# A two-layer retention and latent-attention trunk on one core: x's HBM copy, the place of the sines, the place of the scores, and two jobs moved from VectorE to ScalarE

## The chip, the core and the metric

The kernel runs on one core of a Trainium2 chip. The core has a matrix engine (TensorE), a vector engine (VectorE), an engine for activation functions and scaled copies (ScalarE), a general engine (GpSimd), and a queue that issues most transfers (SyncE, called SP in the profile). They run beside each other, each works through its own instructions in order, and they wait for one another with semaphores. In the profile they are PE (with PEld for its weight loads), ACT, DVE, POOL and SP. The metric is the time of one execution on the device in microseconds. The kernel before was run three times: 2519.52, 2520.91 and 2526.63 us, so the median is 2520.91 us.

## The reference, cut to what matters

The input x has 256 rows of 2048 numbers (float32). Two layers follow each other, and each is followed by an MLP of width 8192.

```python
# layer 0: retention, 8 heads, qk 256, v 512
h = rms_norm(x, norm_mix[0])
q, k, v, gate = split(h @ w_in)
q, k = apply_rope(q, cos, sin), apply_rope(k, cos, sin) * 256**-0.5
o = (q @ k.T * decay) @ v                 # written by chunks in the reference
o = o * rsqrt(mean(o * o) + eps)
x = x + (silu(gate) * o) @ w_out
x = x + square(relu(rms_norm(x) @ w1)) @ w2
# layer 1: latent attention, 16 heads, 128 plain + 64 rotary columns
k_nope, k_pe, v = mla_shared_kv(rms_norm(x, kv_norm_in), ...)
q = rms_norm(h @ w_dq) @ w_uq             # then split, normed, rotary part turned
sc = (q_nope @ k_nope.T + q_pe @ k_pe.T) * 192**-0.5      # causal mask
x = x + softmax(sc) @ v @ w_o
x = x + square(relu(rms_norm(x) @ w1)) @ w2
```

The angles of the rotation are positions times fixed frequencies; their sines and cosines are computed on the chip.

## The kernel before

All weights are float32 and are streamed from HBM once. Each float32 factor of a product is split into a rounded part (`wh`) and a remainder (`wl`): `split` rounds by a copy on ScalarE (L167, or L170 with a scale) and subtracts on VectorE (L168, L171). A product then is three matmuls: high by high, high by low, low by high. `stream` (and `quad` for the large products, which uses a seven-product scheme for some blocks) loads one chunk of a weight on SP into one of 3 `raw` buffers, splits it into two halves of 1024 columns, and issues the matmuls. There are 5 buffers for each kind of half. So the chain for each half is SP, ScalarE, VectorE, TensorE.

Work beside the weight stream is put off with `later(n, fn)`: `fn` runs when n more chunks have been issued (a chunk is one tick of `clock`), and `tick` calls what is due. The framework's scheduler then gives each engine its order from the order of issue and from its own estimate of when operands are ready; so an instruction can stand earlier on its engine than where it was written. Small tiles of 2 KB per partition come from one pool, `f2k`, with 14 buffers; whoever takes a buffer waits for the last reader of its former content.

The start runs as follows. `start(half)` is called for each half of the first weight (gate of head 0, `rg`); it loads two blocks of the transposed x (`x0t`) and splits them into `act0`, scaled by the norm's gain. The norm's row scale isn't known yet: the first products are made without it, and the rotation tables and gates take it up. At half 5, `ret_tables` lets GpSimd compute the reduced angles (`sincos`, L465 to L501: `tr_ang` to `tr_rr`, some twenty instructions). At half 7 the following is put off: `load_x` loads x itself in eight tiles of 128x512 on SP (`x0`) and squares them on ScalarE (`square_sum`, L162); `scale_tables` (`later(5)`) makes the row scales `r0` (sums on VectorE, power on GpSimd, L145 and L147), takes the sines of the angles on ScalarE (L505), multiplies them by `r0` (`tr_scaled`, L540) and transposes them on TensorE (`tr_tp`) into `rope_tab`; `mla_tables` takes the sines of the second layer's angles (`tm`); and eight copies of x from HBM to HBM (`xh`, the running x's home) are issued by GpSimd (L594).

For each head h, `ret_projected` streams the query and the key weights (`rq`, `rk`, 2 chunks each). `ret_rope` adds the two parts of the product (L600, L601) and later rotates (`rotate`, L607 to L611); `ret_scores` later multiplies keys by queries (`sc`, L626), multiplies by the decay (`st`, L628 and L629) and splits (`sh`, `sl`). Head 0's values (`rv`, 4 chunks) come next, and for later heads gate and values together (`rp`, 8 chunks); then `ret_out` multiplies the split scores with the split values (`vh`, `vl`, L170 and L171). Head 0 has to wait for the tables, so its rotations, scores and gate are put off by more ticks (`wait`, L679).

In layer 1, the query stage streams `uq` in three chunks for each of eight pairs of heads. `query` copies the product from PSUM with the row scale (`qs`, ScalarE, L942), squares it (`qu`, VectorE, L944), sums the squares (L945, L946), norms and turns; after transposes (`qntp`, `qptp`), `score` multiplies with the keys, masks (L999), takes the maximum (L1004), the exponential with its sum (ScalarE, L1009), the reciprocal (L1010) and multiplies by it (VectorE, L1015). Its result is transposed (`ptp`) and multiplied by the values (`ao`), and the output product `wo` follows.

Of the kernel before, what the change touches and what calls it, by code (L numbers as in the profile page):

```python
# [15 lines left out]
AF = mybir.ActivationFunctionType  # L16
ALU = mybir.AluOpType
# [4 lines left out]
NT = 2  # L22
# [3 lines left out]
NB = 4  # L26
# [24 lines left out]
def yoco(ctx: ExitStack, tc: tile.TileContext, a):  # L51
# [7 lines left out]
    def small(w, name):  # L59
        return pool.tile([P, w], F32, tag="small", bufs=36, name=name)  # L60
# [20 lines left out]
    def later(n, fn):  # L81
        queue.append((clock[0] + n, next(count), fn))
# [77 lines left out]
    def square_sum(src, acc, name):  # L160
        junk = pool.tile([P, 512], BF16, tag="junk", bufs=1, name=f"{name}_sq")
        nc.scalar.activation(junk[:, : src.free_size()], src, AF.Square, accum_out=acc)  # L162
# [302 lines left out]
    def sincos(inv, w, name):  # L465

        n = NT * w

        def f2k(shape, name):
            return shaped(act_tile(name, F32).rearrange("p j i s -> p (j i s)"), shape)  # L470

        ang = f2k([NT, w], f"{name}_ang")
        for t in range(NT):
            nc.gpsimd.tensor_scalar(ang[:, t], inv, pos_f[:, t : t + 1], None, op0=ALU.mult)
        flat = ang.rearrange("p t w -> p (t w)")
        k = f2k([2, n], f"{name}_k")
        for i in range(2):
            nc.gpsimd.tensor_scalar(k[:, i], flat, 1 / (2 * PI), 0.25 * i, op0=ALU.mult, op1=ALU.add)
        nc.gpsimd.tensor_scalar(k, k, MAGIC, -MAGIC, op0=ALU.add, op1=ALU.add)
        kh = f2k([2, n], f"{name}_kh")  # L480
        nc.gpsimd.tensor_scalar(kh, k, MAGIC_HI, -MAGIC_HI, op0=ALU.add, op1=ALU.add)
        kl = f2k([2, n], f"{name}_kl")
        nc.gpsimd.tensor_tensor(kl, k, kh, op=ALU.subtract)
        r = f2k([2, n], f"{name}_rr")
        both = flat.unsqueeze(1).to_broadcast([P, 2, n])
        part = f2k([2, n], f"{name}_part")

        def less(dst, src, kk, c):
            nc.gpsimd.tensor_scalar(part, kk, c, None, op0=ALU.mult)
            nc.gpsimd.tensor_tensor(dst, src, part, op=ALU.subtract)  # L490

        less(r, both, kh, c1)
        for kk, c in ((kl, c1), (kh, c2), (kl, c2), (k, c3)):
            less(r, r, kk, c)
        nc.gpsimd.tensor_scalar(r[:, 1], r[:, 1], PI / 2, None, op0=ALU.add)
        nc.gpsimd.tensor_scalar(k, r, 1 / (2 * PI), MAGIC, op0=ALU.mult, op1=ALU.add)
        nc.gpsimd.tensor_scalar(k, k, -MAGIC, None, op0=ALU.add)
        for c in (c1, c2 + c3):
            less(r, r, k, c)
        lim = 3.1415925  # L500
        nc.gpsimd.tensor_scalar(r, r, lim, -lim, op0=ALU.min, op1=ALU.max)  # L501

        def finish():
            sc = f2k([2, n], f"{name}_sc")
            nc.scalar.activation(sc, r, AF.Sin)  # L505
            return sc.rearrange("p i (t w) -> p i t w", t=NT)

        return finish
# [4 lines left out]
    gqn = pool.tile([P, 1], F32, name="gqn")  # L513

    def mla_tables():
        sm = mla_sc[0]()
        for t in range(NT):
            for i, s in ((0, 1.0), (1, scale)):
                tab = pe_tabs[t][i]
                g = gpe[:, i * ROPE : (i + 1) * ROPE]  # L520
                for half in range(2):
                    cols = slice(half * 32, half * 32 + 32)
                    other = slice(32 - half * 32, 64 - half * 32)
                    nc.vector.scalar_tensor_tensor(
                        tab[:, 0, cols], sm[:, 1, t], s, g[:, cols], op0=ALU.mult, op1=ALU.mult
                    )
                    nc.vector.scalar_tensor_tensor(
                        tab[:, 1, cols], sm[:, 0, t], s * (2 * half - 1), g[:, other], op0=ALU.mult, op1=ALU.mult
                    )
# [4 lines left out]

    def scale_tables():
        r0.extend(x_rstd(ss0, "n0"))
        sc = ret_sc[0]()
        scaled = f2k([2, NT, P], "tr_scaled")
        for t in range(NT):
            nc.vector.tensor_scalar(scaled[:, :, t], sc[:, :, t], r0[t], None, op0=ALU.mult)  # L540

        def turn():
            nc.scalar.copy(rope_tab, transposed(lambda t, j: scaled[:, j, t], "tr_tp"))

        later(2, turn)


    act0, sums0, r0, ret_sc, mla_sc = [], [], [], [], []

    def first_inputs(c):  # L550

# [17 lines left out]
    def x_in(t, b):  # L569
        return a["x"][t * P : (t + 1) * P, b * 512 : (b + 1) * 512]  # L570

    def load_x(b):
        for t in range(NT):
            x0 = f2k([512], f"x0_{t}{b}")
            nc.sync.dma_start(x0, x_in(t, b))
            square_sum(x0, ss0[t][:, b : b + 1], f"n0_{t}{b}")

    def start(half):
        first_inputs(half)
        if half == 3:  # L580
            nc.sync.dma_start(pos_i, a["pos"])
            nc.sync.dma_start(cst, a["cst"])
            nc.sync.dma_start(gpe, a["gpe"])
        if half == 5:
            ret_tables()
        if half == 7:
            for b in range(NB):
                later(2 + b, lambda b=b: load_x(b))
            later(5, scale_tables)
            later(12, lambda: mla_sc.append(sincos(cst[:, C_INVM : C_INVM + 32], 32, "tm")))  # L590
            later(20, mla_tables)
            for b in range(NB):
                for t in range(NT):
                    later(20 + b, lambda t=t, b=b: nc.gpsimd.dma_start(x_home[t][b], x_in(t, b)))  # L594

    def ret_rope(acc, out, name, wait):

# [78 lines left out]

    def ret_projected(h, qk, gate, v, s):

        wait = 0 if h else 7  # L679

        def keyed(acc):
            ret_rope(acc, qk, f"rk{h}", max(wait - 4, 0))
            later(max(wait - 4, 0) + 1, ret_scores(h, qk, s))

        gemm_t(a["ret_w_qk"], h * 2, act0, KD, f"rq{h}", lambda acc: ret_rope(acc, qk, f"rq{h}", max(wait - 2, 0)))
        gemm_t(a["ret_w_qk"], (RH + h) * 2, act0, KD, f"rk{h}", keyed)
# [22 lines left out]
    for h in range(RH):  # L709
        qk, gate, v, s = [], [], [], []  # L710
        if h == 0:

            def gated(acc, gate=gate):
                src = [f2k([512], f"gate_raw{t}") for t in range(NT)]
                for t in range(NT):
                    nc.scalar.copy(src[t], acc[t])

                def silu():
                    for t in range(NT):
                        g = f2k([512], f"gate0{t}")  # L720
                        nc.scalar.activation(g, src[t], AF.Silu, scale=r0[t])
                        gate.append(g)

                later(7, silu)

            gemm(a["ret_w_gv0"], 0, act0, KD, 512, "rg0", gated, start)
            ret_projected(h, qk, gate, v, s)
            gemm(
                a["ret_w_gv0"], 4, act0, KD, 512, "rv0",
                lambda acc, v=v, s=s, gate=gate: ret_valued(acc, 0, s, v, gate),  # L730
            )
            continue
# [12 lines left out]
        while None in [sums0[k] for k in SEVEN]:  # L745
            run_first()
        gemm_pair(a["ret_w_gv"], (h - 1) * 8, list(zip(act0, sums0)), [k in SEVEN for k in range(8)], f"rp{h}", paired)
# [189 lines left out]
    def query(acc, b):  # L937
        qr, qu = [], []
        sq = small(4 * NT, f"sq{b}").rearrange("p (t i h) -> p t i h", t=NT, i=2)
        for t in range(NT):  # L940
            q = f2k([2, 192], f"qs{b}{t}")
            nc.scalar.activation(q.rearrange("p h c -> p (h c)"), acc[t], AF.Copy, scale=rq[t])  # L942
            u = f2k([2, 192], f"qu{b}{t}")
            nc.vector.tensor_tensor(u, q, q, op=ALU.mult)  # L944
            nc.vector.reduce_sum(sq[:, t, 0], u[:, :, 0:NOPE], axis=AX.X)  # L945
            nc.vector.reduce_sum(sq[:, t, 1], u[:, :, NOPE:], axis=AX.X)  # L946
            qu.append((q, u))
# [31 lines left out]
    def score(b, qt, qpe):  # L979
# [31 lines left out]
        for t in range(NT):  # L1011
            for hh in range(2):
                i = 2 * t + hh
                view = p[t][:, hh]
                nc.vector.tensor_scalar(view, view, inv[:, i : i + 1], None, op0=ALU.mult)  # L1015

        def turn():
            pt = []
# [128 lines left out]
```

## Time and profile before

| | us |
|---|---|
| median of three runs | 2520.91 |
| the profiled execution's own time | 2515.45 |
| its span, first to last instruction | 2513.7 |
| TensorE busy | 2475.7 |
| VectorE busy | 2062.4 |
| ScalarE busy | 1532.9 |
| GpSimd busy | 236.8 |

The granted clock of TensorE was 0.997 over the whole span. The profile puts the busy times of each engine beside the span. A row of a timeline gives the start and the length in microseconds from the span's start, the engine, the line of the kernel, the operation, the tile written and the tiles read with their shapes, and in brackets how long the engine stood before it and what released it. A row of the waits gives who waited for whom: the sum in microseconds, the number of times, the longest. A row of a stretch gives busy time (and count) for TensorE, its weight loads, VectorE, ScalarE and GpSimd, then the granted clock, the busy share of the DMA engines and the GB/s that they moved. A row of a tile or line gives the count and the duration in nanoseconds (least, median, most) and where it started first and last. A row of the transfers gives who issues them, how many, their size and the median time from issue to landing in microseconds.

### The profile page before, as it was taken

The page shows a single profiled execution, that of the slowest core. Times are in us where ns is not written, and L with a number is a line of the kernel's source. Part 1 is how long each engine was busy: PE and PEld are TensorE (multiplying, and loading weights), DVE is VectorE, ACT ScalarE, POOL GpSimd, SP SyncE. Part 2 cuts the span into 40 slices and gives each one's busy share as a digit, 9 for nine tenths or more (in the row PEclk, how much of TensorE's full clock was granted, in tenths as well). Part 3 has the DMA queues.
Part 4 walks back from the last instruction along what each step waited for, and adds up shares of the span by engine and source line. Part 5 has one row for each costly group of instructions (what it writes and reads, how often), then busy time and mean ns, then how long its engine had stood idle before and what let it go on. Part 6 is the DMA issues. An engine that isn't in the chain of part 4 may idle for free.

```text
span 2513.7 us, 31410 instructions
## 1 busy us (share of the span) xinstructions
PE 2475.7 (98%) x11704; PEld 2077.5 (83%) x11704; DVE 2062.4 (82%) x2692; ACT 1532.9 (61%) x2138; POOL 236.8 (9%) x307
## 2 busy tenths in 40 slices
PE   6999999999999999999999999999999999999999
PEld 5888888888888888888888888998888888888887
DVE  4788888887888988888889866887689888888896
ACT  4555655555567656657566666565566566575663
POOL 6300001000000020010110011101000201101100
PEclk9999999999999999999999999999999999999999
DMA  6645458555555586685775565435555866857754
GB/s 235 221 176 192 170 196 259 196 195 203 198 195 203 197 257 203 211 253 187 242 245 211 204 210 180 164 126 201 184 186 195 263 207 209 250 197 235 248 207 165
DMA packets 92824, 519.97 MB, mean 207 GB/s; under 512 B 11008, under 2 KB 12160, under 8 KB 39424
## 3 DMA queue, kind: packets, MB, share of 16 engines
q1 hardware_dynamic: 71280, 471.78, 52.4%
q0 software_dynamic: 21248, 46.15, 8.8%
q8 instruction: 91, 1.49, 0.2%
q14 instruction: 61, 0.50, 0.1%
q10 hardware_dynamic: 144, 0.05, 0.0%
HBM read 480.18 MB, written 39.85 MB: 207 GB/s over the span
## 4 chain that ended last, share of the span: by engine, by line
PE 83%; DVE 7%; DMA 4%; ACT 3%; POOL 2%; issue 1%; SPq 0%; ACTq 0%; DVEq 0%; POOLq 0%
PE u_c L337 7%; PE u_c L338 7%; PE u_c L336 7%; PE d_c L337 5%; PE d_c L338 5%; PE d_c L336 5%; PE rp_c L338 3%; PE rp_c L337 3%; PE rp_c L336 3%; PE ro_c L337 2%; PE ro_c L338 2%; PE ro_c L336 2%; PE u_p L338 2%; PE u_p L337 2%; PE u_p L336 2%; DMA d_raw<-in_mlp_w 2%
## 5 line engine op out<-in xcount | busy, mean ns | idle before, releaser
L168 DVE TENSOR_TENSOR u_wl<-u_raw,u_wh 128x1024 fp32r<-128x1024 f32 (+1 forms) x256 | 279.5, 1122 | 41.0 <-ACT u_wh L167 40.7
L168 DVE TENSOR_TENSOR d_wl<-d_raw,d_wh 128x1024 fp32r<-128x1024 f32 (+1 forms) x256 | 283.4, 1132 | 26.4 <-ACT d_wh L167 25.4
L336 PE MATMUL u_c<-u_wh,n 128*128 128x512 f32 x742 | 290.4, 391 | 0.0
L337 PE MATMUL u_c<-u_wl,n 128*128 128x512 f32 x742 | 288.9, 389 | 0.3 <-DVE u_wl L168 0.3
L338 PE MATMUL u_c<-u_wh,n 128*128 128x512 f32 x742 | 288.9, 389 | 0.0
L167 ACT CAST u_wh<-u_raw 128x1024 fp32r<-128x1024 f32 (+1 forms) x256 | 239.0, 980 | 72.4 <-PE u_c L338 30.7
L167 ACT CAST d_wh<-d_raw 128x1024 fp32r<-128x1024 f32 (+1 forms) x256 | 239.8, 990 | 56.5 <-DMA d_raw<-in_mlp_w 25.5
L337 PE MATMUL d_c<-d_wl,hid 128*128 128x512 f32 x644 | 251.4, 390 | 1.6 <-DVE d_wl L168 1.6
L336 PE MATMUL d_c<-d_wh,hid 128*128 128x512 f32 x644 | 252.0, 391 | 0.0
L338 PE MATMUL d_c<-d_wh,hid 128*128 128x512 f32 x644 | 250.9, 390 | 0.0
L167 ACT CAST u_wh<-u_u 128x1024 fp32r<-128x1024 f32 x94 | 96.2, 1050 | 157.0 <-DVE u_u L301 124.9
L167 ACT CAST d_wh<-d_u 128x1024 fp32r<-128x1024 f32 x84 | 84.9, 1049 | 162.3 <-DVE d_u L301 154.6
L337 PEld LDWEIGHTS u_c<-u_wl,n 128*128 128x128 f32 x742 | 139.4, 188 | 29.4 <-DVE u_wl L168 1.0
L338 PEld LDWEIGHTS u_c<-u_wh,n 128*128 128x128 f32 x742 | 139.3, 188 | 29.0
L336 PEld LDWEIGHTS u_c<-u_wh,n 128*128 128x128 f32 x742 | 139.3, 188 | 28.3
L167 ACT CAST rp_wh<-rp_raw 128x1024 fp32r<-128x1024 f32 x112 | 106.9, 972 | 75.0 <-PE rp_c L338 45.5
L168 DVE TENSOR_TENSOR u_wl<-u_u,u_wh 128x1024 fp32r<-128x1024 f32 x94 | 113.1, 1222 | 46.7 <-ACT u_wh L167 46.6
L337 PEld LDWEIGHTS d_c<-d_wl,hid 128*128 128x128 f32 x644 | 120.9, 188 | 28.8 <-DVE d_wl L168 4.2
L338 PEld LDWEIGHTS d_c<-d_wh,hid 128*128 128x128 f32 x644 | 120.9, 188 | 24.9
L336 PEld LDWEIGHTS d_c<-d_wh,hid 128*128 128x128 f32 x644 | 120.9, 188 | 24.7
L168 DVE TENSOR_TENSOR d_wl<-d_u,d_wh 128x1024 fp32r<-128x1024 f32 x84 | 99.8, 1222 | 35.9 <-ACT d_wh L167 35.9
L168 DVE TENSOR_TENSOR rp_wl<-rp_raw,rp_wh 128x1024 fp32r<-128x1024 f32 x112 | 121.7, 1120 | 8.0 <-ACT rp_wh L167 6.4
(470 smaller groups left out, 6400.3 us busy)
## 6 DMA issues: line engine op xcount, KB each, us to landing
u_raw<-in_mlp_w SPq DMA_DIRECT2D x128, 1024.0 KB, 5.4
d_raw<-in_mlp_w SPq DMA_DIRECT2D x112, 1024.0 KB, 4.9
rp_raw<-in_ret_w_gv SPq DMA_DIRECT2D x56, 1024.0 KB, 4.9
ro_raw<-in_ret_w_out SPq DMA_DIRECT2D x32, 1024.0 KB, 4.9
uq_raw<-in_mla_w_uq SPq DMA_DIRECT2D x24, 768.0 KB, 4.2
rq_raw<-in_ret_w_qk SPq DMA_DIRECT2D x16, 1024.0 KB, 6.2
rk_raw<-in_ret_w_qk SPq DMA_DIRECT2D x16, 1024.0 KB, 4.9
d_raw<-in_mlp_w2t SPq DMA_DIRECT2D x16, 1024.0 KB, 5.1
```

What stands on the lines that cost most here:

```text
L167: nc.scalar.copy(h, src)
L168: nc.vector.tensor_tensor(l, src, h.bitcast(F32), op=ALU.subtract)
L336: nc.tensor.matmul(dst, ah, bh, start=n == 0, stop=False)
L337: nc.tensor.matmul(dst, ah, bl, start=False, stop=False)
L338: nc.tensor.matmul(dst, al, bh, start=False, stop=n == total[key] - 1)
```

## The change

Four things change.

1. The eight copies of x from HBM to HBM go. In their place each x tile, once loaded for its squares, is written from SBUF to x's home by a DMA that GpSimd issues.
2. The sines take a bias: a column of zeros which GpSimd makes by multiplying the second row block's scale `r0[1]` by 0. So the sine can't stand ahead of the norm's scale. `scale_tables` is put off by 6 ticks and not 5, head 0's rotations, scores and gate by one tick more.
3. In heads 1 to 7 the scores are made two ticks after the keys, not one.
4. In the query stage ScalarE makes the squares straight from PSUM with the row scale, in place of VectorE's product; and ScalarE multiplies the exponentials by the reciprocal in place of VectorE.

```diff
-        def finish():
+        def finish(zero):
             sc = f2k([2, n], f"{name}_sc")
-            nc.scalar.activation(sc, r, AF.Sin)
+            nc.scalar.activation(sc, r, AF.Sin, bias=zero)
...
-        sm = mla_sc[0]()
+        sm = mla_sc[0](no_turn[0])
...
         r0.extend(x_rstd(ss0, "n0"))
-        sc = ret_sc[0]()
+        zero = small(1, "no_turn")
+        nc.gpsimd.tensor_scalar(zero, r0[1], 0.0, None, op0=ALU.mult)
+        no_turn.append(zero)
+        sc = ret_sc[0](zero)
...
             square_sum(x0, ss0[t][:, b : b + 1], f"n0_{t}{b}")
+            nc.gpsimd.dma_start(x_home[t][b], x0)
...
-            later(5, scale_tables)
+            later(6, scale_tables)
...
-            for b in range(NB):
-                for t in range(NT):
-                    later(20 + b, lambda t=t, b=b: nc.gpsimd.dma_start(x_home[t][b], x_in(t, b)))
...
-        wait = 0 if h else 7
+        wait = 0 if h else 8
...
-            later(max(wait - 4, 0) + 1, ret_scores(h, qk, s))
+            later(max(wait - 4, 0) + (2 if h else 1), ret_scores(h, qk, s))
...
-                later(7, silu)
+                later(8, silu)
...
-            nc.vector.tensor_tensor(u, q, q, op=ALU.mult)
+            nc.scalar.activation(u.rearrange("p h c -> p (h c)"), acc[t], AF.Square, scale=rq[t])
...
-                nc.vector.tensor_scalar(view, view, inv[:, i : i + 1], None, op0=ALU.mult)
+                nc.scalar.activation(view, view, AF.Copy, scale=inv[:, i : i + 1])
```

More of the change, by code (lines that the diff above doesn't have):

```diff
@@ L545, in scale_tables @@
         later(2, turn)
-    act0, sums0, r0, ret_sc, mla_sc = [], [], [], [], []
+    act0, sums0, r0, ret_sc, mla_sc, no_turn = [], [], [], [], [], []
     def first_inputs(c):
```

## The prediction

> **What bounds the kernel now.** I read the page's head first, then the list of who waited for whom on TensorE, then the first 130 us and the query stage instruction by instruction.
>
> ```profile
> span 2513.7 us, 31410 instructions
> ...
> PE 2475.7 (98%) x11704; PEld 2077.5 (83%) x11704; DVE 2062.4 (82%) x2692; ACT 1532.9 (61%) x2138; POOL 236.8 (9%) x307
> ```
>
> TensorE works for 2475.7 us, and the edits leave its matmuls as they are. Only its idle 38.0 us (2513.7 − 2475.7), and time in which its clock is low, can be won. The waits of TensorE, longest first, say where it idles (sum, times, longest):
>
> ```profile
> PE rk_acc L256 <- ACT rk_wh L167: 9.7, 1, 9.7
> PE rg_acc L228 <- ACT a L170: 7.7, 3, 5.6
> PE sc L626 <- DVE rk_q L610: 6.7, 4, 3.7
> ...
> PE qptp L187 <- DVE ot L168: 1.3, 2, 0.9
> PE qptp L187 <- ACT qt L969: 1.2, 1, 1.2
> ```
>
> The edits aim at the first and third rows, touch the second by the way, and the last two a little. The largest wait, in the timelines of ScalarE, GpSimd and TensorE:
>
> ```profile
> 40.16 1.28 ACT L505 ACT_TABLE_LOAD   x1
> 57.19 0.63 ACT L505 ACTIVATE tr_sc<-tr_rr 128x512 f32<-128x512 f32 x1 [15.74 <-POOL tr_rr L501]
> 56.54 0.61 POOL L501 TENSOR_SCALAR tr_rr<-tr_rr 128x512 f32<-128x512 f32 x1
> 36.57 0.63 PE L256 MATMUL rq_acc<-a,rq_wh 128*128 128x512 f32 x2
> 48.33 0.40 PE L256 MATMUL rq_acc<-a,rq_wh 128*128 128x512 f32 x1
> 48.69 0.39 PE L256 MATMUL rq_acc<-a,rq_wh 128*128 128x512 f32 x1
> 58.80 0.80 PE L256 MATMUL rk_acc<-a,rk_wh 128*128 128x512 f32 x1 [9.73 <-ACT rk_wh L167]
> 61.30 0.63 PE L256 MATMUL rk_acc<-a,rk_wh 128*128 128x512 f32 x1
> 61.94 0.63 PE L256 MATMUL rk_acc<-a,rk_wh 128*128 128x512 f32 x1
> 73.07 0.40 PE L228 MATMUL rv_acc<-rv_wh,a 128*128 128x512 f32 x1
> ```
>
> ScalarE stands 15.74 us in front of the first sine, whose angles GpSimd finishes at 57.15. Behind it on ScalarE are the weight casts (L167) that feed TensorE, which therefore stands for 9.73 us. It then restarts slowly: 0.64 us from one pair (512 and 256 columns) to the next at 61.30, against 0.36 at 48.33. The key GEMM has 32 such pairs, so at full rate 32 × 0.36 = 11.5 us; it took 73.07 − 58.80 = 14.3, 2.8 us more.
>
> **The change part by part.**
>
> *Term A, x's copy to HBM.* Eight DRAM-to-DRAM copies at the very start of GpSimd's queue go away; eight writes from SBUF come later.
>
> ```profile
> q0 software_dynamic: 640, 2.10, 15.3%
> ACT rg_wh L167 <- DMA rg_raw<-in_ret_w_gv: 6.8, 6, 2.1
> 10.00:12.00 2.00, 0.50 (x3) 0.06 (x1) 0.96 (x1) 1.21 (x2) 0.00 (x0) 1.00 1.03 406
> 18.57 1.05 ACT L167 CAST rg_wh<-rg_raw 128x1024 fp32r<-128x1024 f32 x1 [0.50 <-DMA rg_raw<-in_ret_w_gv]
> ```
>
> The first row is the first 40 us: GpSimd's queue moved 2.10 MB in 15.3% of the 16 engines' time, 6.1 us. Those engines are full (1.03 of their time between 10 and 12 us, the last column but one), and ScalarE waits for weights until 18.57, so the copies push the first loads back. Without them this point comes up to 6.1 us earlier. From there to 36.57 TensorE is nearly gapless, so the gain is kept. I take −5.0 us; ends −6.1 and −1 (if VectorE's shares or SP's own waits pace the start instead).
>
> *Term B, the sines behind the norm's scale.* The sine gets a bias made from r0, so its place on ScalarE moves behind all eight squares of x, after the first cast of the last value chunk; the casts of the key GEMM no longer queue behind GpSimd. TensorE then runs from queries into keys. Gone: 9.7 us of standing and 2.8 us at the slow rate, 12.5. What is late next is GpSimd's angles, which nobody needs until the transposes of the sines, placed now right before the last value chunk. The added GpSimd multiplication and the wait for it hide under the table load of 1.28 us. I take −12.2, since nothing else on ScalarE is late by then; ends −12.5 and −9.7 (the rate stays low for another reason).
>
> The Trainium skill ("TensorE: Matmul & The Clock Gate", Part 1: The HAM clock gate) says that an idle window of about 3.4 us halves the clock and a busy one restores it. The trace agrees in kind (9.73 us idle, then pairs at 0.64 instead of 0.36); by its 3.4 us the slow stretch would cost 1.7 instead of 2.8, and term B would be −11.1.
>
> What the new order can hold up: the SBUF writes stand on GpSimd behind the angles, and the load of x's last two tiles takes buffers that the first two writes must free; SP has the next weights queued behind these loads.
>
> ```profile
> 77.88 0.63 ACT L162 ACTIVATE n_sq<-x 128x512 bf16<-128x512 f32 x1 [0.81 <-DMA x<-in_x]
> 81.13 0.39 DVE L540 TENSOR_SCALAR tr_scaled<-tr_sc,n_r 128x256 f32<-128x256 f32 x1 [0.95 <-POOL n_r L147]
> xh<-x_ro POOLq DMA_DIRECT2D x8, 256.0 KB, 4.8
> x_ro<-xh POOLq DMA_DIRECT2D x8, 256.0 KB, 3.3
> xh<-ro_v POOLq DMA_DIRECT2D x2, 256.0 KB, 11.1
> ```
>
> With the start 5 us earlier the angles end near 52; a first write issued at 52.5 lands after 4.8 us at 57.3, and the last x loads land after 3.3 at about 61. From the last squares to the end of the scaling took 3.6 us before (77.88 to 81.52), and the sine adds 0.63 and its hand-overs, some 5 us: 66. TensorE reaches the transposes after the keys and 72 matmuls of three value chunks, 0.24 each (two thirds of a pair): 44 + 11.5 + 17.3 = 73. So at least 6 us of cover; at the slowest write seen on that queue, 11.1 us, still none is lost. SP's held-up queries of head 1 are due only when the values end, near 78. Cost: nothing.
>
> The Trainium skill ("DMA: Bandwidth & Descriptors", SWDGE vs HWDGE vs iDMA) warns that VectorE can lock GpSimd out while it writes descriptors, which speaks against writes issued amid VectorE work. The trace's 3.3 to 11.1 us for this queue include such stages; the cover stands at either.
>
> *Term C, a new wait in head 0.* Both rotations now stand on VectorE behind the two value remainders (vl) and the first key remainder of head 1, all of which wait for the end of the value GEMM; before, they were done by 92.1, ahead of the scores at 95.33.
>
> ```profile
> 86.77 0.77 DVE L607 TENSOR_TENSOR rq_q<-rq_u,rope_tab 128x512 f32<-128x512 f32 x1
> 91.50 0.68 DVE L611 TENSOR_TENSOR rk_q<-rk_q,rk_v 128x256 f32<-128x256 f32 x1
> 94.85 1.37 ACT L170 ACTIVATE vh<-rv_acc,n_r 128x512 fp32r<-128x512 f32 x2 [0.98 <-PE rv_acc L230]
> 95.33 1.47 PE L626 MATMUL sc<-rq_q,rk_q 128*128 128x256 f32 x8
> 96.11 1.04 ACT L167 CAST rk_wh<-rk_raw 128x1024 fp32r<-128x1024 f32 x1
> 97.23 0.41 DVE L628 TENSOR_TENSOR st<-sc,dec 128x256 f32<-128x256 f32 x1
> 97.76 1.24 DVE L168 TENSOR_TENSOR rk_wl<-rk_raw,rk_wh 128x1024 fp32r<-128x1024 f32 x1
> 98.92 0.64 DVE L168 TENSOR_TENSOR sl<-st,sh 128x384 fp32r<-128x384 f32 x1
> ```
>
> From the end of the values: two vh 1.37, cast 1.04, remainder 1.24, rotations up to 5.4 (86.77 to 92.18, with GpSimd busy beside them): 9.0 us. TensorE gets to the scores after 19 pairs, 6.8 us: a wait of 2.2, less if the rotations run faster. Then only some 2.3 us of matmuls stand between the scores and the first product with them, while scaling and splitting took 97.23 to 99.56, again 2.3, with more queued between: up to 1 us. I take +2.7; ends 0 and +5 (head 0's gate, with its table load of 1.28 us, also moves ahead of two key casts).
>
> *Term D, scores one tick later in heads 1 to 7.* They stand one row pair later, 24 matmuls of 0.24 or 5.8 us, which is more than any wait:
>
> ```profile
> 629.22 0.67 PE L626 MATMUL sc<-rq_q,rk_q 128*128 128x256 f32 x2 [3.69 <-DVE rk_q L610]
> ```
>
> This one is the longest of the four (6.7 in all). The matmuls that take its place use weights already split, and the score's readers come whole row pairs later. I take −6.2; ends −6.7 and −4.5, if part of it is handed to the next weight remainder.
>
> *Term E, query squares and softmax scaling on ScalarE.* Eight head pairs, each like this window and these rows (ns: least, median, most):
>
> ```profile
> 1660.20:1678.03 17.83, 16.96 (x111) 16.52 (x110) 15.27 (x42) 10.42 (x23) 1.64 (x1) 1.00 0.38 133
> L944 DVE TENSOR_TENSOR qu<-qs x16: 547/552/559, 1602.1 to 1719.9; 128x384 f32<-128x384 f32 x16
> L1015 DVE TENSOR_SCALAR p<-p,inv x32: 279/319/353, 1642.9 to 1762.5; 128x128 f32<-128x128 f32 x16, 128x256 f32<-128x256 f32 x16
> L942 ACT ACTIVATE qs<-uq_acc,cq_r x16: 562/582/584, 1601.5 to 1717.1; 128x384 f32<-128x384 f32 x16
> L1009 ACT ACTIVATE p<-p,mx x32: 384/448/498, 1640.8 to 1761.0; 128x128 f32<-128x128 f32 x16, 128x256 f32<-128x256 f32 x16
> ```
>
> VectorE loses 2 × 0.55 + 4 × 0.32 = 2.4 us per pair, ScalarE gets 2 × 0.58 + 4 × 0.45 = 3.0: 12.9 and 13.4 of 17.83. Neither becomes the bound, but TensorE already is (16.96, in other pairs all of it), so nearly nothing is won: at most the 2.5 us of qptp waits. Behind the scaling, which waits for VectorE's reciprocal, stand weight casts, with 7.4 us of ScalarE's idle time as cover. I take −1.0; ends −2.5 and +3.
>
> **Sum:** −5.0 − 12.2 + 2.7 − 6.2 − 1.0 = −21.7 us. The profiled execution took 2515.45 us, so 2493.8 there. It lies 5.5 under the median of the runs shown, 2520.91; against that, 2499.2, which is my number.
>
> **The rivals.**
> - The start is not freed (term A zero): VectorE's splits or SP's waits pace it. For: ScalarE's largest single DMA wait is only 2.1 us. Against: the full DMA engines. −16.7: 2504.
> - The score waits only move on to the next weight remainder (term D zero). For: VectorE is 82% busy. Against: the next weights are already split there. −15.5: 2505.
> - ScalarE becomes the feeder that is late in the query stage: each in-order wait for the reciprocal holds the casts. If all of the added 3.0 us per pair came through, 24 us, in place of term E, the gain would be eaten: −20.7 + 24 = +3.3, 2524, no change. Against: 7.4 us idle per pair.
> The Trainium skill ("ScalarE: Activation LUTs", Rules for kernel authors) says to keep multiplications on VectorE, not ScalarE. The trace agrees on the single instruction (0.32 against 0.45).
> - Slower: the first write to HBM lands so late that x's last loads, the norm and the sines hold TensorE at the transposes and SP's weights with them. Each microsecond beyond the 6 of cover costs one; to end 0.3% slower it must land 6 + 21.7 + 7.6 = 35 us later than at 57.3, after some 40 us of flight, against 11.1 for the slowest above. The price at that point is 2528.
>
> **How the numbers follow.** About 0.3%, 7.6 us, is what a measurement here can tell from no change. Forecast 0.67, start not freed 0.11, waits moved on 0.10, ScalarE late 0.07, slower 0.05. The first three are faster by over 0.3%: 0.88; same 0.07; slower 0.05. The best ends sum to −6.1 − 12.5 + 0 − 6.7 − 2.5 = −27.8 (2493), the worst to −1 − 9.7 + 5 − 4.5 + 3 = −7.2 (2514). Runs differ by some 5 us, as the profiled one shows, so the range is 2490 to 2510: the forecast and the next two rivals, with 0.2 or less outside.
>
> **What would show it.** A: the first query matmul near 31.5. B: no ScalarE wait for the angles and no slow pairs in the key GEMM; values begin near 55. C: a wait of TensorE for the rotation in head 0, some 2 us. D: no waits at sc in heads 1 to 7. E: query pairs still 17.8 us long. Wrong would be: TensorE waiting at the transposes of the sines, or at weights whose DMA SP issued late around 60, or pairs of the query stage longer than 18 us.

## The result and the profile after

| | before | after |
|---|---|---|
| median of the runs, us | 2521.43 (4 runs, 2519.52 to 2526.63) | 2497.84 (4 runs, 2493.58 to 2499.82) |
| the profiled execution's own time, us | 2515.45 | 2497.18 |
| its span, us | 2513.7 | 2495.2 |
| TensorE idle in it, us | 38.0 | 22.7 |

The ratio is 0.9901, with a 95% interval of 0.9881 to 0.9921: 23.6 us faster by the medians, 18.5 by the spans of the two profiles. The head of the page after, and TensorE's waits after (sum, times, longest):

```profile
span 2495.2 us, 31419 instructions
...
PE 2472.5 (99%) x11704; PEld 2077.2 (83%) x11704; DVE 2047.9 (82%) x2644; ACT 1549.9 (62%) x2186; POOL 245.8 (10%) x308
```

```profile
PE rg_acc L228 <- ACT a L170: 5.3, 1, 5.3
PE d_c L337 <- DVE d_wl L168: 4.2, 6, 1.1
PE qptp L187 <- DVE ot L168: 1.9, 1, 1.9
...
PE sc L627 <- DVE rk_q L611: 1.3, 1, 1.3
```

The 9.7 us ahead of the keys are gone, of the four waits at the scores one is left (head 0's, a new one), and the start's three waits are one. Two rows have grown most: the MLP's remainders (d_wl, 1.6 before) and the wait of the query stage for the first attention output (ot, two waits of 1.3 together before). TensorE's busy time fell by 3.2 us though its matmuls are the same: that is slow clock that went (granted 0.999 over the span, 0.997 before).

Where the time went is best read from the first matmul of each stage in the two timelines of TensorE:

| first matmul of | before | after | after − before | change within the stage ahead of it |
|---|---|---|---|---|
| queries of head 0 (rq) | 36.57 | 30.83 | −5.74 | −5.74, term A |
| keys (rk) | 58.80 | 42.97 | −15.83 | −10.09, term B |
| values (rv) | 73.07 | 54.26 | −18.81 | −2.98, term B |
| first seven-product block of head 1 (rp_p) | 139.88 | 123.87 | −16.01 | +2.80, term C |
| first MLP (u_c) | 755.05 | 731.64 | −23.41 | −7.40, term D |
| query stage (uq) | 1588.27 | 1566.94 | −21.33 | +2.08, no edit |
| last transposes at the start of the second MLP (n_tp) | 1830.76 | 1810.80 | −19.96 | +1.37, term E |
| end of the span | 2513.7 | 2495.2 | −18.5 | +1.5, no edit |

The edits alone come to −5.74 − 13.07 + 2.80 − 7.40 + 1.37 = −22.0 us. The other 3.6 us were given back in stages that no edit touches; the last part of the experiments bears on them.

The start and the sines after, in the timelines of TensorE, ScalarE and VectorE:

```profile
30.83 0.61 PE L256 MATMUL rq_acc<-a,rq_wh 128*128 128x512 f32 x2
42.97 0.39 PE L256 MATMUL rk_acc<-a,rk_wh 128*128 128x512 f32 x1
43.31 0.40 PE L256 MATMUL rk_acc<-a,rk_wh 128*128 128x512 f32 x1
70.59 0.60 PE L187 MATMUL tr_tp<-cst,tr_scaled 128*128 128x128 f32 x4
61.99 0.63 ACT L162 ACTIVATE n_sq<-x 128x512 bf16<-128x512 f32 x1 [3.76 <-DMA x<-in_x]
67.06 0.72 ACT L505 ACTIVATE tr_sc<-tr_rr,no_turn 128x512 f32<-128x512 f32 x1 [1.00 <-POOL no_turn L538]
67.82 0.70 DVE L543 TENSOR_SCALAR tr_scaled<-tr_sc,n_r 128x256 f32<-128x256 f32 x2 [1.80 <-ACT tr_sc L505]
```

Queries run into keys without a stop (42.97 has no bracket) and the key pairs keep 0.34 us (42.97 to 43.31). The sine stands behind x's squares, and ScalarE's 3.76 us for x's last load now fall where TensorE does not need it. But it was close: the scaled sines are done at 68.52 and TensorE asks for them at 70.59.

Head 0 after, in the timelines of VectorE and TensorE:

```profile
76.74 1.43 DVE L171 SCALAR_TENSOR_TENSOR vl<-rv_acc,n_r,vh 128x512 fp32r<-128x512 f32 x2 [0.32 <-ACT vh L170]
78.35 1.24 DVE L168 TENSOR_TENSOR rk_wl<-rk_raw,rk_wh 128x1024 fp32r<-128x1024 f32 x1 [0.18 <-ACT rk_wh L167]
80.39 0.69 DVE L608 TENSOR_TENSOR rq_q<-rq_u,rope_tab 128x512 f32<-128x512 f32 x1 [0.79 <-ACT gate L722]
84.53 0.51 DVE L612 TENSOR_TENSOR rk_q<-rk_q,rk_v 128x256 f32<-128x256 f32 x1
84.66 1.57 PE L627 MATMUL sc<-rq_q,rk_q 128*128 128x256 f32 x8 [1.32 <-DVE rk_q L611]
88.72 0.50 PE L646 MATMUL o<-vh,sh 128*128 128x512 f32 x1 [0.27 <-ACT sh L167]
107.63 0.50 PE L336 MATMUL rp_c<-rp_wh,a 128*128 128x512 f32 x1 [0.49 <-DVE rk_u L602]
```

The chain that was predicted stands there: value remainders, key remainder, rotations, scores. One link was not foreseen: the first rotation also stands 0.79 us for the gate.

### The profile page after: what moved, and what is told of

Its sections match the earlier page's. It is cut to its first block, busy times and chain, and to the rows that moved or that the text cites. A ratio compares the mean times of both kernels' runs of the same rounds, so it can differ in the third digit from the quotient of the medians.

```text
span 2495.2 us, 31419 instructions
## 1 busy us (share of the span) xinstructions
PE 2472.5 (99%) x11704; PEld 2077.2 (83%) x11704; DVE 2047.9 (82%) x2644; ACT 1549.9 (62%) x2186; POOL 245.8 (10%) x308
## 3 DMA queue, kind: packets, MB, share of 16 engines
q8 instruction: 91, 1.49, 0.2%
## 4 chain that ended last, share of the span: by engine, by line
PE 84%; DVE 8%; ACT 4%; DMA 3%; issue 1%; POOL 0%; ACTq 0%; SPq 0%; DVEq 0%; POOLq 0%
PE u_c L337 7%; PE u_c L338 7%; PE u_c L336 7%; PE d_c L337 4%; PE d_c L338 4%; PE d_c L336 4%; PE rp_c L337 3%; PE rp_c L338 3%; PE rp_c L336 3%; DVE d_wl L168 3%; PE rq_acc L256 2%; PE rk_acc L256 2%; DMA d_raw<-in_mlp_w 2%; PE ro_c L337 2%; PE ro_c L336 2%; PE ro_c L338 2%
## 5 line engine op out<-in xcount | busy, mean ns | idle before, releaser
L168 DVE TENSOR_TENSOR u_wl<-u_raw,u_wh 128x1024 fp32r<-128x1024 f32 (+1 forms) x256 | 279.2, 1120 | 43.2 <-ACT u_wh L167 42.9
L168 DVE TENSOR_TENSOR d_wl<-d_raw,d_wh 128x1024 fp32r<-128x1024 f32 (+1 forms) x256 | 283.0, 1130 | 30.6 <-ACT d_wh L167 29.7
L168 DVE TENSOR_TENSOR u_wl<-u_u,u_wh 128x1024 fp32r<-128x1024 f32 x94 | 113.0, 1222 | 46.2 <-ACT u_wh L167 46.2
L168 DVE TENSOR_TENSOR d_wl<-d_u,d_wh 128x1024 fp32r<-128x1024 f32 x84 | 99.8, 1221 | 35.9 <-ACT d_wh L167 35.9
L336 PE MATMUL rp_c<-rp_wh,a 128*128 128x512 f32 x322 | 126.5, 393 | 0.5 <-DVE rk_u L602 0.5
```

Of the source, the lines that this page charges most:

```text
L168: nc.vector.tensor_tensor(l, src, h.bitcast(F32), op=ALU.subtract)
L336: nc.tensor.matmul(dst, ah, bh, start=n == 0, stop=False)
```

## The experiments

Each kernel below is the changed kernel with the edits that its section shows, and was timed beside the kernel before. That kernel's medians beside them were 2521.81, 2521.72 and 2520.63 us. The changed kernel itself was not timed again, so differences of one or two microseconds between rows say little; stages are compared by their profiles.

| run | median, us | ratio to before, 95% interval |
|---|---|---|
| changed kernel | 2497.84 | 0.9901 (0.9881 to 0.9921) |
| copies to HBM as before | 2503.12 | 0.9930 (0.9915 to 0.9944) |
| sixteen extra copies | 2513.12 | 0.9955 (0.9938 to 0.9971) |
| sines not tied | 2509.34 | 0.9959 (0.9946 to 0.9972) |
| scores one tick behind keys | 2506.46 | 0.9944 (0.9929 to 0.9959) |
| squares and scaling on VectorE | 2495.18 | 0.9902 (0.9883 to 0.9920) |
| scaling on VectorE | 2491.93, again 2494.00 | 0.9876 (0.9861 to 0.9890), again 0.9898 (0.9880 to 0.9917) |
| squares on VectorE | 2501.58 | 0.9918 (0.9903 to 0.9933) |
| head 0's scores later | 2497.25 | 0.9898 (0.9883 to 0.9912) |
| scaling on VectorE, gate earlier | 2494.49 | 0.9897 (0.9883 to 0.9912) |

### Term A: the copies at the start

Undone:

```diff
-            nc.gpsimd.dma_start(x_home[t][b], x0)
...
+            for b in range(NB):
+                for t in range(NT):
+                    later(20 + b, lambda t=t, b=b: nc.gpsimd.dma_start(x_home[t][b], x_in(t, b)))
```

> The changed kernel with part 1 undone: x's copy to HBM is again eight HBM-to-HBM copies, which stand first on GpSimd's queue; the rest stays as changed. My theory (the copies take DMA time from the first weight loads): the first query matmul goes back from 30.8 to about 36.5 us and nothing after it makes that good, since TensorE is nearly gapless from there: 2497.8 + 5.7 = 2503.5 us. Rival 1 (the start came earlier for another reason, the copies are hidden): 30.8 stays, 2498. Rival 2 (the writes from SBUF cost as much later as the copies did at the start, by holding x's last loads): the time stays near 2498 although the first query matmul is at 36.5, since x's squares then end earlier.

Doubled, with sixteen copies into unused places and the writes from SBUF kept:

```diff
+    x_more = [[dram.tile([P, 512], F32, name=f"xm_{t}_{b}") for b in range(8)] for t in range(NT)]
...
+            for b in range(8):
+                for t in range(NT):
+                    later(20 + b, lambda t=t, b=b: nc.gpsimd.dma_start(x_more[t][b], x_in(t, b % NB)))
```

> The changed kernel with sixteen HBM-to-HBM copies of x's tiles into unused places, first on GpSimd's queue; the writes from SBUF stay. Twice the suspected cost of part 1. My theory (the copies take DMA time from the first weight loads in proportion to their bytes): the first query matmul goes from 30.8 by 2 x 5.7 to 2 x 8.1 us (the two sizes that eight copies showed) to 42 to 47 us, and the end with it: 2497.8 + 11.5 to 16 = 2509 to 2514. Rival 1 (a fixed cost of having such copies first in the queue): as with eight, 37 to 39 us and 2503. Rival 2 (the copies fill gaps of a limited number of transfers in flight, so that more of them only run longer): between 39 and 42, 2503 to 2508.

Measured: 2503.12 and 2513.12 us. Undone: the first query matmul in the timeline; GpSimd's queue in the first 40 us (packets, MB, share of the engines' time); and the stretch from 5 to 30 us:

```profile
38.89 0.62 PE L256 MATMUL rq_acc<-a,rq_wh 128*128 128x512 f32 x2
```

```profile
q0 software_dynamic: 640, 2.10, 15.6%
```

```profile
5.00:30.00 25.00, 19.93 (x57) 14.74 (x58) 13.88 (x24) 13.98 (x27) 7.34 (x9) 0.80 0.98 333
```

Doubled, the first two of these:

```profile
47.51 0.39 PE L257 MATMUL rq_acc<-a,rq_wh 128*128 128x512 f32 x1
```

```profile
q0 software_dynamic: 1280, 4.20, 30.3%
```

And the changed kernel's stretch beside them:

```profile
5.00:30.00 25.00, 24.35 (x93) 19.04 (x94) 19.57 (x29) 17.32 (x34) 13.15 (x11) 1.00 0.97 339
```

Eight copies move the start by 8.1 us and sixteen by 16.7 (from 30.83): one microsecond for each in the changed kernel, so it is no fixed cost. They take 6.2 and 12.1 us of all DMA engines' time (15.6% and 30.3% of 40 us). ScalarE's waits for the first weight and for x0t grow with them, from 4.7 us in the changed kernel to 11.8 and 17.2, and were 10.4 before, where the same eight copies cost 5.7 us. So the price goes with the number of copies, and comes by way of late loads. That leaves 1 to 4 us, which a slower TensorE fits: its granted clock is 0.80 between 5 and 30 us with eight copies, 0.93 there and 0.83 in the ten microseconds after with sixteen, 0.93 in the kernel before, and 1.00 in the changed kernel. That the clock is the rest is argued. Both rivals fall; most of it stays to the end (7.2 us in the profile, 5.3 by the medians).

### Term B: the sines

```diff
-        def finish(zero):
+        def finish():
...
-            nc.scalar.activation(sc, r, AF.Sin, bias=zero)
+            nc.scalar.activation(sc, r, AF.Sin)
...
-        nc.gpsimd.tensor_scalar(zero, r0[1], 0.0, None, op0=ALU.mult)
...
```

> The changed kernel without the bias of the sines, so that nothing ties them to the norm's scale; the ticks stay as changed. On ScalarE the sine then stands ahead of the first cast of the key weights again. My theory: GpSimd's angles end near 53.6 as in the changed kernel, the queries end near 43, so TensorE stands some 12 us ahead of the key GEMM (it starts near 55.2) and then runs it at the slow rate for 2.8 us more; up to 2.8 us of the waits in head 0 go in exchange, since the rotation table is early against the values: +12.3 + 2.8 - 2.5 = +12.6, 2510.5 us. So part 1 without part 2 would be worth only the 3.5 us by which the angles end earlier. Rival 1 (the slow stretch has another reason than the standing): no more than +9.8, 2507.6, with the wait but pairs of matmuls at 0.36 us after it. Rival 2 (x's last loads, for which ScalarE stands 3.8 us at 62 us in the changed kernel, are what paces this stage in either order): within 3 us of 2498.

Measured: 2509.34 us, 11.5 above the changed kernel; 12.0 by the spans. The sine, and TensorE behind it:

```profile
51.09 0.63 ACT L505 ACTIVATE tr_sc<-tr_rr 128x512 f32<-128x512 f32 x1 [15.73 <-POOL tr_rr L501]
52.71 0.80 PE L256 MATMUL rk_acc<-a,rk_wh 128*128 128x512 f32 x1 [9.73 <-ACT rk_wh L167]
56.48 0.63 PE L256 MATMUL rk_acc<-a,rk_wh 128*128 128x512 f32 x1
57.12 0.47 PE L256 MATMUL rk_acc<-a,rk_wh 128*128 128x512 f32 x1
57.54 0.39 PE L256 MATMUL rk_acc<-a,rk_wh 128*128 128x512 f32 x1
```

The wait of 9.73 us is back to the hundredth, and so is the slow stretch: 0.64 us a pair at 56.48, 0.42 at 57.12. The values start at 66.44 in place of 54.26, 12.2 later, and the end of head 0 is 12.7 later. The expectation had the sum right and two parts wrong. GpSimd's angles end at 51.05, not at 53.6, so the wait is 9.7 and not 12: GpSimd takes 35.3 us for them (from 15.77) and not 37.5 (from 16.13). VectorE has nothing at all to do here between 42 and 51 us, while it is busy for 8.4 of 11 us from 42 to 53 in the changed kernel; that this is the reason is likely and not shown. And none of head 0's waits went in exchange (1.6 us at the scores). So part 1 is worth its 6 us without part 2 as well (rv at 66.44 against 73.07 before), and the two add up. Both rivals fall: the slow stretch came with the stop, and the time did not stay within 3 us of the changed kernel's.

### Term D: the scores one tick nearer

```diff
-            later(max(wait - 4, 0) + (2 if h else 1), ret_scores(h, qk, s))
+            later(max(wait - 4, 0) + 1, ret_scores(h, qk, s))
```

> The changed kernel with part 3 undone: the scores of heads 1 to 7 one tick after the keys. My theory: TensorE waits for the rotated keys again in heads 2, 3, 4 and 7, some 6.7 us in all, with up to 0.7 us of refilling after them: 2497.8 + 7.4 = 2505.2 us. Rival 1 (the waits were handed on to the remainders of the next weights): time as changed, 2498, with these waits in the trace and fewer elsewhere. Rival 2 (the waits depend on how the stage before falls, and with head 0 moved they fall otherwise): other heads, between 2 and 10 us.

Measured: 2506.46 us, 8.6 above the changed kernel. Of TensorE's waits, the row of the scores:

```profile
PE sc L627 <- DVE rk_q L611: 8.3, 6, 3.0
```

Head 0's wait is 1.6 of the 8.3; the other five are at heads 2, 3, 4, 6 and 7 (1.8, 0.9, 0.8, 0.2 and 3.0). From the first joint chunk to the first MLP the kernel loses 9.15 us. The waits were not handed on: outside head 0 they come to 6.7 us, as before the change. Rival 2 is right in so far as their sizes shift. Some 2.5 us more are not explained by a wait; in the ten profiles with the scores later, the stretch from head 1's first seven-product block to the first MLP alone varies from 607.8 to 610.5 us (615.2 before, 616.7 here).

### Term E: squares and scaling

Both undone:

```diff
-            nc.scalar.activation(u.rearrange("p h c -> p (h c)"), acc[t], AF.Square, scale=rq[t])
+            nc.vector.tensor_tensor(u, q, q, op=ALU.mult)
...
-                nc.scalar.activation(view, view, AF.Copy, scale=inv[:, i : i + 1])
+                nc.vector.tensor_scalar(view, view, inv[:, i : i + 1], None, op0=ALU.mult)
```

> The changed kernel with part 4 undone: squares of the queries and softmax scaling on VectorE. What the two traces suggest: in the second pair of heads of the query stage TensorE's wait at qptp falls back from 1.9 to 0.9 us and the 2.5 us at the slow rate behind it go, later pairs lose up to 1.2 us in exchange: net 1.4 us faster, 2496.4. Rival 1 (as I predicted: the part is worth 1.0 us, and the wait in the second pair is a matter of that one execution): 2498.8. Rival 2 (ScalarE is the late feeder in this stage): pairs shorter than now, more than 5 us faster, below 2493. A side question in all four: the MLP stages, which no part touches, took 2.1 and 1.5 us longer in the profile of the changed kernel than before it. If that is a matter of the single execution, their lengths scatter over these four by 1 to 3 us without regard to the edit; if the changed kernel's order causes it, all four show 651.6 and 684.4 us.

Only the second edit (the scaling back on VectorE):

> The changed kernel with the softmax scaling back on VectorE; the squares stay on ScalarE. In the changed kernel ScalarE's four scalings (1.5 us together) stand behind the exponentials and ahead of a weight cast and the cast of the first attention output, and TensorE stands 1.9 us in the second pair for the remainder of that output. My theory: the scaling alone makes the second pair's wait; it falls to 0.8 or 0.9 us as before the change, with no slow stretch behind it: query stage 242.4 us instead of 243.9, 2496.4 in all. Rival (the squares, which stand between the row-scaled copies and the next casts, make it): 1.9 us and 2497.8 stay.

Only the first (the squares back on VectorE):

> The changed kernel with the query squares back on VectorE; the scaling stays on ScalarE. My theory (the scaling makes the wait): 1.9 us at qptp in the second pair as in the changed kernel, in some executions with a slow stretch of 1.0 to 1.5 us behind it; query stage 242.3 to 243.9 us, 2497.8 in all. Rival (the squares make it): 0.9 us, 242.4 and 2496.4.

Measured: 2495.18, 2491.93 and 2501.58 us. The length of the query stage (first uq matmul to the last transposes at the start of the second MLP) by what ScalarE does in it:

| | nothing moved | squares | scaling | both |
|---|---|---|---|---|
| query stage, us | 242.43, 242.49 | 239.27, 239.25, 239.31 | 248.98 | 242.31 to 245.75 |

The first column is the run with both undone and the kernel before, the second three profiles of two kernels, the third one profile, the last the six kernels with both. So one half of the edit is worth −3.2 us, and the other +6.5 alone (6.4 by the medians, 2501.58 against 2495.18) and +4.6 beside the squares (243.86 in the changed kernel). With both undone the theory held (2496.4 expected, and a wait of 0.9 us in place of 1.9 that measured 0.8). With one half undone, theory and rival both missed: they had the stage between 242.3 and 243.9 us. The waits of TensorE in the pairs of this stage, first with the scaling on VectorE and the squares on ScalarE:

```profile
PE qptp L187 <- ACT qt L970: 0.4, 1, 0.4
```

with only the scaling on ScalarE:

```profile
PE qptp L187 <- DVE ot L168: 3.5, 3, 1.9
PE qptp L187 <- ACT qt L970: 2.6, 1, 2.6
...
PE ao L1034 <- ACT pt L1025: 1.7, 1, 1.7
```

These sum to 7.8 us, against 2.7 with nothing moved: 5.1 of the 6.5 us. Behind the stop of 2.6 us the granted clock was 0.69 for 4 us, which fits the rest.

How the scaling does it stands where the changed kernel scales the second pair's exponentials. The pairs overlap there: the first pair's attention output is split and the fourth pair's queries are transposed at the same time. Below are the timelines of VectorE, ScalarE and TensorE, and the stretches from the fourth pair's transposes to the fifth's and from there to the sixth's:

```profile
1637.83 0.18 DVE L1011 RECIPROCAL inv<-den 128x4 f32<-128x4 f32 x1 [0.53 <-ACT p L1010]
1637.70 0.82 ACT L167 CAST uq_wh<-uq_raw 128x768 fp32r<-128x768 f32 x1
1638.43 1.49 ACT L1016 ACTIVATE p<-p,inv 128x128 f32<-128x128 f32 x4
1639.82 0.82 ACT L167 CAST uq_wh<-uq_raw 128x768 fp32r<-128x768 f32 x1
1640.55 0.57 ACT L167 CAST ot<-ao 128x512 fp32r<-128x512 f32 x1
1641.55 0.68 DVE L168 TENSOR_TENSOR ot<-ao,ot 128x512 fp32r<-128x512 f32 x1
1642.29 1.10 PE L187 MATMUL qptp<-cst,qpp 128*128 128x128 f32 x4 [1.89 <-DVE ot L168]
```

```profile
1639.80:1661.21 21.41, 19.52 (x115) 19.09 (x114) 15.96 (x38) 15.02 (x33) 2.31 (x1) 0.92 0.44 148
1661.21:1678.91 17.70, 17.70 (x115) 17.50 (x114) 12.66 (x35) 12.67 (x29) 2.31 (x1) 1.00 0.34 113
```

Four scalings of 1.49 us together stand in ScalarE's order ahead of a weight cast and of the cast of the attention output (ot). That cast starts 2.72 us after the reciprocal; in the kernel before it was 1.33:

```profile
1658.98 0.18 DVE L1010 RECIPROCAL inv<-den 128x4 f32<-128x4 f32 x1 [0.53 <-ACT p L1009]
1660.31 0.57 ACT L167 CAST ot<-ao 128x512 fp32r<-128x512 f32 x1
```

The transposes wait until its remainder (L168) has been made, since the kernel puts both results into the same two PSUM banks (`tp`), the memory that TensorE writes to. ScalarE is free for 6.4 of the 21.41 us of this stretch; the free time does not lie here. The same stretch took 18.80 us in the kernel before and 17.91 with the squares alone on ScalarE.

The Trainium skill ("ScalarE: Activation LUTs", Rules for kernel authors) puts multiplications on VectorE. The runs agree for the scaling and disagree for the squares: a square by ScalarE takes 0.574 us against 0.552 on VectorE, and yet moving the sixteen squares is worth 3.2 us. It takes 1.1 us per pair off VectorE; that the transposes come sooner for that reason is argued from the waits that went (2.7 us at qptp and ao with all on VectorE, 0.4 with the squares moved), and from pairs of 17.70 in place of 17.83 us.

The version with only the scaling undone has the lowest median, so it was run once more:

> The changed kernel with the softmax scaling on VectorE, once more, as the neighbour of the run with the early gate, and as a second profile of one and the same kernel. My theory: 2491.9 again within 1.5 us, query stage 239.3 us within 0.5; the stages that no edit touches differ between its two profiles by 1 to 2 us (first MLP 650.6 before), which would be the scatter of a single execution. Rival (the query stage's gain of 4.6 us over the changed kernel was a lucky execution): 242 to 244 us again, 2495 to 2497.

Measured: 2494.00 us, query stage 239.25 against 239.27. By the medians it is 5.9 and 3.8 us under the changed kernel, by this stage 4.6. The intervals of the whole times overlap (again 0.9880 to 0.9917, the changed kernel 0.9881 to 0.9921), so it is the stage that shows the gain.

### Term C: head 0

Two attempts to win the new wait back. Scores and the product with the values one tick later in head 0:

```diff
-            later(max(wait - 4, 0) + (2 if h else 1), ret_scores(h, qk, s))
+            later(max(wait - 4, 0) + 2, ret_scores(h, qk, s))
...
-        later(1, lambda: ret_out(h, s, v, gate, halves[h // 4]))
+        later(1 if h else 2, lambda: ret_out(h, s, v, gate, halves[h // 4]))
```

> The changed kernel with head 0's scores one tick later (after all 64 matmuls of the next head's query GEMM and not after 38 of them) and its product with the values one tick later too. My theory: the wait that the change made in head 0 (1.3 us at the scores, 0.3 at the product behind them) has 26 matmuls, 6 us, more of cover and goes; the 0.5 us at the first product of the joint gate and value chunk stays: 2497.8 - 1.6 = 2496.2 us, values to the first joint chunk 49.5 us instead of 51.1. Rival 1 (the wait is only moved to the next row pair, since VectorE has head 1's remainders to do as well): 51.1 us stay, 2498. Rival 2 (the outputs of head 0 come so late that the gate and value chunks behind them wait for PSUM): slower by 1 to 3 us, 2500.

And, on top of the scaling on VectorE, the gate earlier, since the rotations stood for its buffer:

```diff
-                later(8, silu)
+                later(7, silu)
```

> The changed kernel with the softmax scaling on VectorE, and head 0's gate one tick earlier (7 in place of 8). In the changed kernel the rotations of head 0 start at 80.4 us on VectorE, behind two value remainders, a key remainder and 0.8 us of standing for the gate, whose raw copy gives up its buffer when ScalarE has read it; TensorE waits 1.3 to 1.5 us at the scores for them. With the earlier gate its table load and two activations (2.6 us) stand behind the sine on ScalarE, where TensorE waits for nothing for 3 us, and the rotations stand right behind the value remainders. My theory: the rotations start near 78.2, the wait at the scores goes, 1.5 us won against the version with the scaling on VectorE alone (2491.9): 2490.4; values to the first joint chunk 49.7 us instead of 51.2. Rival 1 (the wait goes on to the product behind the scores, as when the scores stood later): 51.2 and 2491.9 stay. Rival 2 (the 2.6 us on ScalarE hold the cast of the last value weights): a new wait in the value GEMM of 1 to 2 us, values longer than 22.2 us, 2493.

Measured: 2497.25 and 2494.49 us; nothing won. The stretch from the values to the first joint chunk took 50.9 and 51.5 us, against 51.1 in the changed kernel and 51.3 and 51.5 in the two profiles with the scaling on VectorE. With the scores later:

```profile
94.73 0.49 PE L646 MATMUL o<-vh,sh 128*128 128x512 f32 x1 [1.67 <-ACT sh L167]
112.07 1.57 PE L627 MATMUL sc<-rq_q,rk_q 128*128 128x256 f32 x8 [0.96 <-DVE y L168]
```

With the gate earlier:

```profile
72.80 5.34 DVE L168 TENSOR_TENSOR rq_wl<-rq_raw,rq_wh 128x1024 fp32r<-128x1024 f32 x4
79.39 0.68 DVE L608 TENSOR_TENSOR rq_q<-rq_u,rope_tab 128x512 f32<-128x512 f32 x1
83.92 1.57 PE L627 MATMUL sc<-rq_q,rk_q 128*128 128x256 f32 x8 [1.60 <-DVE rk_q L611]
```

In the first the wait only moves to the product, and from there to head 1's scores: rival 1. In the second the gate's 2.6 us on ScalarE push the casts of head 1's query weights back, VectorE's four remainders then stand in one block until 78.1, and the rotations start at 79.4, 1.0 us earlier and not 2.2. The scores also stand six matmuls earlier in TensorE's order (after 32 of the query GEMM and not 38), and wait 1.6 us. So the wait hangs on VectorE's whole queue behind the values, not on the one buffer. That was neither the theory nor one of its rivals.

### The stages that no edit touches

The first MLP's length (first u_c matmul to the first transposes of the next layer) in twelve profiles, in which no edit reaches it: 647.65 to 651.62 us, 649.53 before, 651.62 after. The second MLP: 633.7 to 637.6, 633.7 before, 635.2 after (from the last transposes to the first matmul of its last block). One kernel profiled twice gave 650.61 and 649.13 in the first. So the 3.6 us that the table above shows as given back lie within the scatter of single executions; that the changed order adds nothing there at all is not shown, and in the second MLP the kernel before is the shortest of the twelve.

## Why the prediction was right, and where it was not

Predicted were 2499.2 us in a range of 2490 to 2510, faster; measured 2497.84. By its steps:

- **A**, −5.0 with ends −6.1 and −1: −5.7, first query matmul at 30.83 against "near 31.5". That the copies held the start is shown by the two doses, eight and sixteen. The rival (start not freed) falls. Undoing it in the changed kernel costs 8.1 us at the start, 1.9 more than the DMA time of the copies; the step counted DMA time alone, and the clock of 0.80 there is the likely rest, which is not shown.
- **B**, −12.2 with ends −12.5 and −9.7: −13.1, a little beyond the end: keys 10.09 (9.73 of standing, the rest in the query GEMM) and 2.98 of slow clock, priced at 2.8. The cover was mis-sized: "at least 6 us" was 2.1 (68.52 to 70.59). The sines were ready 2.5 us later than the 66 worked out: GpSimd's angles ended at 53.6 and not near 52, so x's last squares stood at 63.1 and not near 61. The table load was to hide the wait for GpSimd's zero column; ScalarE stood 1.00 us more for it. And TensorE came 2.4 us earlier than 73, since the keys started at 43 and not 44 and 72 value matmuls took 16.3 us and not 17.3. No price came of it: the writes to HBM landed 3.8 to 6.7 us after their issue, in line with the 4.8 reckoned with. But the slower rival, built on that margin, was nearer than its working made it.
- **C**, +2.7: +2.8. The place and the chain were right; the parts were 1.3 at the scores (2.2 predicted), 0.3 at the product (up to 1) and 0.5 at the first joint chunk, which was not foreseen; 0.7 is not named by any wait.
- **D**, −6.2 with ends −6.7 and −4.5: −7.4, and 8.6 when undone. The mechanism was right: at heads 1 to 7 no wait at the scores is left, so the rival (the waits move on) falls. The 0.7 us beyond the 6.7 of waits lie within the scatter of this stage (607.8 to 610.5 us in ten profiles with the scores later, against 615.2 before), so no step of the sum is shown to be wrong here.
- **E**, −1.0 with ends −2.5 and +3: +1.4. The sign was wrong: five of the six profiles with both halves are 1.4 to 3.3 us longer in this stage than the kernel before, one is 0.2 shorter. The sign that was named for it showed, a pair longer than 18 us: 21.41 at the stop. It was no clean sign, since the same pair took 18.80 before; the window of 17.83 shown as a pair began 0.9 us ahead of that pair's transposes and ended 1.9 ahead of the next. The step that failed is "with 7.4 us of ScalarE's idle time as cover": it took the free time of a whole pair as cover for four instructions at one place of an in-order queue. And the two moves were priced as one: −3.2 for the squares and +4.6 for the scaling beside them nearly cancel. The rival "ScalarE late" had the right mechanism; its 24 us (all of 3.0 in each of eight pairs) stand against 6.5 for the scaling alone.

The sum came out right partly by luck: the five terms miss by −0.7, −0.9, +0.1, −1.2 and +2.4 us, and the misses cancel. Against the profile's own time the change is 18.3 us and not 21.7, because the two profiled executions differ by 3.6 us in stages that no edit touches. Against the medians it is 23.6: the profiled execution before lay 6.0 us under its median, the one after only 0.7. So the time met the forecast more closely than the profiles do.

## What to carry to other kernels

An edit that moves two jobs should be priced and run as two: here one half was a gain of 3.2 us and the other a loss that ate it, and neither showed in the total. Mean idle time is no cover on an engine that works in order: ask what stands directly behind the new instruction, and who waits for that. A stop of TensorE can cost more than its length, by the slow stretch behind it: 2.4 and 3.0 us behind the two stops of 9.73, nothing seen behind the one of 3.69.

## What the runs showed of the hardware

- The clock can drop after a stop of only 1.9 us. The same stop (1.89 to 1.91 us, ahead of the fourth query pair's second transposes) stands in seven profiles. In five of them the granted clock of the following 4 us was 0.57 to 0.71, in two it stayed at 1.00. The stage was 243.9 us long in four of the five and 245.8 in the fifth; of the two, it was 242.3 with both halves of the edit and 249.0 with the scaling alone. Transposes stand right before and behind this stop, and whether they count as work for the clock is not shown. But the stops at head 7's scores stand between plain matmuls: before the change one of 3.69 us (629.22) left the clock at 1.00, and with the scores near one of 3.00 us at the same place brought 0.68 over the following 4 us. The Trainium skill ("TensorE: Matmul & The Clock Gate", Part 1: The HAM clock gate) describes a free-running window of about 3.4 us; that chance decides by the phase agrees with these rows, that it takes a whole idle window does not, since 3.00 us were enough. The changed kernel's stretches of the stop and of the 3.7 us behind it (granted clock third from the end):

```profile
1639.80:1642.29 2.49, 0.60 (x6) 0.36 (x4) 1.62 (x3) 2.49 (x6) 0.00 (x0) 1.00 0.68 234
1642.29:1646.00 3.71, 3.71 (x19) 3.71 (x20) 3.04 (x8) 2.74 (x6) 1.35 (x1) 0.54 0.58 195
```

- GpSimd issued eight copies in a row and then held the ninth until one had landed. With sixteen copies:

```profile
1.28 4.30 POOL L599 DMA_DIRECT2D xm<-in_x  x8 [0.44 <-issue]
6.46 0.53 POOL L599 DMA_DIRECT2D xm<-in_x  x1 [0.87 <-DMA xm<-in_x]
```

Whether the queue or the kernel's own order sets the eight was not tried.
